# Roll of a matrix by 100 columns: head reads and stores with descriptors 4 rows apart

## The chip, the cores and the metric

One core of a Trainium2 chip runs the kernel. The metric is the device time of one execution in microseconds, from a median over runs; lower is better. A profile of one execution stands beside it.

## What is computed

```python
x = np.random.randn(8192, 8192).astype(np.float32)
np.roll(x, 100, axis=1)
```

Every row of 8192 float32 values (32,768 bytes) is rotated to the right by 100 columns. So `out[r, 100:]` is `x[r, :8092]`, and the first 100 columns of a row of the output are the last 100 of the same row of the input. Nothing is calculated; 268.4 MB are read and 268.4 MB are written.

## The kernel before

The shift is s = 100. The kernel rounds it up to a = 128 columns (512 bytes) and has g = a - s = 28. It splits each output row in two.

**The long copies.** Columns 128 to 8191 of the output are columns 28 to 8091 of the input. They go from HBM to HBM directly, in 16 transfers of 512 rows, 32,256 bytes to a row (line 31). Even transfers are issued from SP, odd ones from ACT, eight each, and none of them waits for anything that the kernel computes. Each issuing engine has a DMA queue of its own: in the profile q10 and q1. The 16 DMA engines serve both.

**The heads.** The first 128 columns of every output row take the last 100 columns and the first 28 columns of the same input row. These two pieces are not neighbours in that row, but the last 100 columns of row r-1 and the first 28 of row r are: in memory they are one run of 512 bytes. The kernel therefore reads runs of 512 bytes that straddle the row boundary, and VectorE sorts the pieces out in SBUF. The heads use the third DMA queue, q0, whose transfers POOL (GpSimd) issues.

The 8192 rows are treated in 8 stages of 1024 rows (`m = 8`, line 48; `n_st` = 8). In a stage, partition p of the 128 has the 8 neighbouring rows k\*1024 + p\*8 + j. For a stage k:

- The load on line 65 reads, for each partition, 8 runs of 512 bytes, one row (32 KiB) apart, into `t[:, :8, :]`. Slot j then holds the tail of row j-1 and the head of row j.
- The load on line 66 reads the missing tail, 400 bytes of the partition's last row, into slot 8. It is one descriptor to a partition.
- Stage 0 has no row ahead of it, and uses line 59 (8 tails of 400 bytes to a partition) and line 61 (8 heads of 112 bytes to a partition) in place of these.
- VectorE copies the tails (line 68) and the heads (line 70) from `t` into `h`, which then holds 8 finished runs of 512 bytes.
- The store on line 73 writes them to the 8 neighbouring output rows, again 32 KiB apart.

The order on POOL is loads of stage 0, loads of stage 1, store of stage 0, loads of stage 2, store of stage 1, and so on: a store stands behind the load issued after its own. The pools have a buffer for every stage, so no buffer is reused. POOL's stores wait for the VectorE copies, and the framework has eight completion semaphores for POOL's transfers, so that from the ninth transfer on each also waits for the one eight before it.

Of the kernel before, what the change touches and what calls it, by code (L numbers as in the profile page):

```python
# [1 line left out]

# [4 lines left out]


@with_exitstack
def kernel(  # L10
    ctx: ExitStack,
    tc: tile.TileContext,
    x: bass.AP,
    shift: int,
    out: bass.AP,
):
    nc = tc.nc
    n_rows, n_cols = x.shape
    s = shift % n_cols
    a = -(-s // 128) * 128  # L20
    g = a - s
    P = nc.NUM_PARTITIONS
    engines = [nc.sync, nc.scalar]
    n_chunks = 16
    rows = n_rows // n_chunks


    for i in range(n_chunks):
        r = slice(i * rows, (i + 1) * rows)
        if a < n_cols:  # L30
            engines[i % 2].dma_start(out=out[r, a:], in_=x[r, g:n_cols - s])
    if a == 0:
        return


    if a > 512:
        for i in range(n_chunks):
            r = slice(i * rows, (i + 1) * rows)
            nc.gpsimd.dma_start(out=out[r, :s], in_=x[r, n_cols - s:])
            if g > 0:  # L40
                nc.gpsimd.dma_start(out=out[r, s:a], in_=x[r, :g])
        return

    m = 8
    n_st = n_rows // P // m
    reads = ctx.enter_context(tc.tile_pool(name="reads", bufs=n_st))  # L50
    heads = ctx.enter_context(tc.tile_pool(name="heads", bufs=n_st))
    xt = x.rearrange("(k p j) c -> k p j c", j=m, p=P)
    ot = out.rearrange("(k p j) c -> k p j c", j=m, p=P)
    tiles = []
    for k in range(n_st + 1):
        if k < n_st:
            t = reads.tile([P, m + 1, a], x.dtype)
            if k == 0:
                nc.gpsimd.dma_start(out=t[:, 1:, :s], in_=xt[k, :, :, n_cols - s:])  # L59
                if g > 0:  # L60
                    nc.gpsimd.dma_start(out=t[:, :m, s:], in_=xt[k, :, :, :g])  # L61
            else:
                lead = bass.AP(tensor=x.tensor, offset=k * P * m * n_cols - s,
                               ap=[[m * n_cols, P], [n_cols, m], [1, a]])
                nc.gpsimd.dma_start(out=t[:, :m, :], in_=lead)  # L65
                nc.gpsimd.dma_start(out=t[:, m, :s], in_=xt[k, :, m - 1, n_cols - s:])  # L66
            h = heads.tile([P, m, a], x.dtype)
            nc.vector.tensor_copy(h[:, :, :s], t[:, 1:, :s])  # L68
            if g > 0:
                nc.vector.tensor_copy(h[:, :, s:], t[:, :m, s:])  # L70
            tiles.append(h)
        if k > 0:
            nc.gpsimd.dma_start(out=ot[k - 1, :, :, :a], in_=tiles[k - 1])  # L73


# [1 line left out]
_INS = ['x', 'shift']  # L77
_OUTS = [((8192, 8192), 'float32')]

_NUMBERS = {'shift': 100}  # L80


# [26 lines left out]
```

## Time and profile before

| | |
|---|---|
| median of 4 runs | 847.57 us (835.31 to 855.29) |
| the profiled execution's own time | 835.31 us |
| its span in the profile | 833.5 us |
| VectorE busy | 6.8 us, 16 instructions |
| POOL busy | 18.7 us, 28 instructions |
| bytes moved by the DMA engines | 272.99 MB, mean 328 GB/s |
| loads of stages 1 to 7 (line 65) | 7 of 512 KB, median 117.5 us from issue to landing |
| tails of stages 1 to 7 (line 66) | 7 of 50 KB, median 123.4 us |
| stores (line 73) | 8 of 512 KB, median 91.0 us |
| the last store issued | at 462.3 us |

The bytes of a transfer from HBM to HBM are counted once as moved, and as one read and one write of HBM. A queue's "share of 16 engines" is the time that its packets took, divided by 16 times the stretch looked at. A packet is what a DMA engine takes from a queue in one go: for the long copies it is one row of 32,256 bytes, for head loads and stores it is mostly 8 descriptors of 512 bytes, which is a partition's 4096 bytes. The 1.8 us between the profiled execution's time and its span lie around the span.

### The profile page before, as it was taken

The numbers are of one execution on the slowest core, as the hardware profiler recorded it, in microseconds if no ns is written. First come the engines' busy times: TensorE is split into PE (matmuls) and PEld (weight loads), VectorE is DVE, ScalarE is ACT, GpSimd is POOL, SyncE is SP. The second block draws the span as 40 slices with busy tenths as digits, with TensorE's granted clock in tenths as the row PEclk, the third lists the DMA queues.
The fourth block names the chain that finished last, engine by engine and source line by source line (L and its number), as shares of the span: only waits on it lengthen the run. The fifth ranks groups of instructions, "written<-read, shape, count | busy, mean of one in ns | idle before, by whom it ended". The sixth has DMA issues, their size and how long they took to land.

```text
span 833.5 us, 111 instructions
## 1 busy us (share of the span) xinstructions
DVE 6.8 (1%) x16; POOL 18.7 (2%) x28
## 2 busy tenths in 40 slices
DVE  0000000000000000000000000000000000000000
POOL 2001000000100100100000000000000000000000
DMA  9999999999999999999999999999999999999995
GB/s 297 343 340 325 336 345 333 337 335 336 328 334 334 339 332 335 337 332 335 330 341 335 339 327 338 327 322 327 333 324 327 325 325 324 325 327 324 324 327 200
DMA packets 10993, 272.99 MB, mean 328 GB/s; under 512 B 641, under 2 KB 641, under 8 KB 2801
## 3 DMA queue, kind: packets, MB, share of 16 engines
q10 hardware_dynamic: 4224, 132.12, 46.5%
q1 hardware_dynamic: 4224, 132.12, 46.4%
q0 software_dynamic: 2544, 8.75, 5.4%
q14 instruction: 1, 0.00, 0.0%
HBM read 268.79 MB, written 268.44 MB: 645 GB/s over the span
## 4 chain that ended last, share of the span: by engine, by line
another core or an unknown queue 35%; issue 15%; DMA 5%; DVE 1%; POOL 0%; POOLq 0%; PEldq 0%
DMA t<-in_x_dram 5%; DVE h L68 0%; POOL out_dram L73 0%; DVE h L70 0%; POOL t L59 0%; POOLq L104 0%; POOL t L66 0%; POOL t L65 0%; PEldq L104 0%; POOLq L73 0%
## 5 line engine op out<-in xcount | busy, mean ns | idle before, releaser
L73 POOL DMA_DIRECT2D out_dram<-h x8 | 6.9, 866 | 443.4 <-DVE h L68 406.5
L65 POOL DMA_DIRECT2D t<-in_x_dram x7 | 6.3, 894 | 0.0
L68 DVE COPY h<-t 128x800 f32<-128x800 f32 x8 | 4.6, 577 | 104.1 <-DMA t<-in_x_dram 104.1
L70 DVE COPY h<-t 128x224 f32<-128x224 f32 x8 | 2.2, 277 | 351.1 <-DMA t<-in_x_dram 351.1
L66 POOL DMA_DIRECT2D t<-in_x_dram x7 | 3.9, 563 | 0.0
L59 POOL DMA_DIRECT2D t<-in_x_dram x1 | 1.0, 1033 | 0.8 <-PEq L104 0.8
L61 POOL DMA_DIRECT2D t<-in_x_dram x1 | 0.9, 894 | 0.0
L90 POOL MEMSET const-float32-0.0<- 128x1 f32 x1 | 0.1, 100 | 0.2 <-issue 0.2
L90 POOL MEMSET const-bfloat16-1.0<- 128x1 bf16 x1 | 0.1, 103 | 0.0
L90 POOL MEMSET const-float32-1.0<- 128x1 f32 x1 | 0.1, 99 | 0.0
L90 POOL MEMSET const-uint8-127<- 128x1 uint8 x1 | 0.1, 99 | 0.0
## 6 DMA issues: line engine op xcount, KB each, us to landing
out_dram<-in_x_dram ACTq DMA_DIRECT2D x8, 16128.0 KB, 407.3
out_dram<-in_x_dram SPq DMA_DIRECT2D x8, 16128.0 KB, 408.2
out_dram<-h POOLq DMA_DIRECT2D x8, 512.0 KB, 91.0
t<-in_x_dram POOLq DMA_DIRECT2D x7, 512.0 KB, 117.5
t<-in_x_dram POOLq DMA_DIRECT2D x1, 400.0 KB, 30.6
t<-in_x_dram POOLq DMA_DIRECT2D x7, 50.0 KB, 123.4
t<-in_x_dram POOLq DMA_DIRECT2D x1, 112.0 KB, 39.5
```

The costliest lines, as they stand in the source:

```text
L59: nc.gpsimd.dma_start(out=t[:, 1:, :s], in_=xt[k, :, :, n_cols - s:])
L61: nc.gpsimd.dma_start(out=t[:, :m, s:], in_=xt[k, :, :, :g])
L65: nc.gpsimd.dma_start(out=t[:, :m, :], in_=lead)
L66: nc.gpsimd.dma_start(out=t[:, m, :s], in_=xt[k, :, m - 1, n_cols - s:])
L68: nc.vector.tensor_copy(h[:, :, :s], t[:, 1:, :s])
L70: nc.vector.tensor_copy(h[:, :, s:], t[:, :m, s:])
L73: nc.gpsimd.dma_start(out=ot[k - 1, :, :, :a], in_=tiles[k - 1])
L90: nc = _bacc.Bacc("TRN2", target_bir_lowering=False, num_devices=1)
```

## The change

The rows of the heads are dealt out in another way. There are 2 stages of 4096 rows in place of 8 of 1024. A partition has 32 rows, k\*4096 + p\*32 + j\*4 + q, with j from 0 to 7 and q from 0 to 3. One transfer moves one q: for each partition 8 runs that lie 4 rows (128 KiB) apart, and from partition to partition 32 rows (1 MiB), where it was 8 rows (256 KiB).

For q = 1, 2, 3 the straddling runs of 512 bytes are read (three loads to a stage, line 61 of the changed kernel). They hold the heads of rows 1 to 3 and the tails of rows 0 to 2 of each group of four. The tails of the fourth rows (400 bytes, line 62) and the heads of the first rows (112 bytes, line 65) are read straight into `h`. VectorE makes two copies to a stage, three times as large as before (lines 63 and 66). No special case for the first rows is left. All loads are issued ahead of all stores; then come 8 stores of 1024 rows each, one for each k and q (line 70). The long copies are untouched.

```diff
-    m = 8
-    n_st = n_rows // P // m
+    Q, J = 4, 8
+    n_st = n_rows // (P * Q * J)
...
-    xt = x.rearrange("(k p j) c -> k p j c", j=m, p=P)
-    ot = out.rearrange("(k p j) c -> k p j c", j=m, p=P)
+    xt = x.rearrange("(k p j q) c -> k q p j c", q=Q, j=J, p=P)
+    ot = out.rearrange("(k p j q) c -> k q p j c", q=Q, j=J, p=P)
     tiles = []
-    for k in range(n_st + 1):
-        if k < n_st:
-            t = reads.tile([P, m + 1, a], x.dtype)
-            if k == 0:
-                nc.gpsimd.dma_start(out=t[:, 1:, :s], in_=xt[k, :, :, n_cols - s:])
-                if g > 0:
-                    nc.gpsimd.dma_start(out=t[:, :m, s:], in_=xt[k, :, :, :g])
-            else:
-                lead = bass.AP(tensor=x.tensor, offset=k * P * m * n_cols - s,
-                               ap=[[m * n_cols, P], [n_cols, m], [1, a]])
-                nc.gpsimd.dma_start(out=t[:, :m, :], in_=lead)
-                nc.gpsimd.dma_start(out=t[:, m, :s], in_=xt[k, :, m - 1, n_cols - s:])
-            h = heads.tile([P, m, a], x.dtype)
-            nc.vector.tensor_copy(h[:, :, :s], t[:, 1:, :s])
-            if g > 0:
-                nc.vector.tensor_copy(h[:, :, s:], t[:, :m, s:])
-            tiles.append(h)
-        if k > 0:
-            nc.gpsimd.dma_start(out=ot[k - 1, :, :, :a], in_=tiles[k - 1])
+    for k in range(n_st):
+        t = reads.tile([P, Q - 1, J, a], x.dtype)
+        h = heads.tile([P, Q, J, a], x.dtype)
+        for q in range(1, Q):
+            lead = bass.AP(tensor=x.tensor, offset=(k * P * J * Q + q) * n_cols - s,
+                           ap=[[J * Q * n_cols, P], [Q * n_cols, J], [1, a]])
+            nc.gpsimd.dma_start(out=t[:, q - 1], in_=lead)
+        nc.gpsimd.dma_start(out=h[:, Q - 1, :, :s], in_=xt[k, Q - 1, :, :, n_cols - s:])
+        nc.vector.tensor_copy(h[:, :Q - 1, :, :s], t[:, :, :, :s])
+        if g > 0:
+            nc.gpsimd.dma_start(out=h[:, 0, :, s:], in_=xt[k, 0, :, :, :g])
+            nc.vector.tensor_copy(h[:, 1:, :, s:], t[:, :, :, s:])
+        tiles.append(h)
+    for k, h in enumerate(tiles):
+        for q in range(Q):
+            nc.gpsimd.dma_start(out=ot[k, q, :, :, :a], in_=h[:, q])
```

## The prediction

> **What bounds the kernel now.** I read the page's slices and queues first, since the kernel computes nothing.
>
> ```profile
> DMA  9999999999999999999999999999999999999995
> ...
> q10 hardware_dynamic: 4224, 132.12, 46.5%
> q1 hardware_dynamic: 4224, 132.12, 46.4%
> q0 software_dynamic: 2544, 8.75, 5.4%
> ...
> HBM read 268.79 MB, written 268.44 MB: 645 GB/s over the span
> ```
>
> The DMA engines are busy in every slice but the last. The heads (q0) are 8.75 of 273 MB and 5.4% of the engine time: 45.0 us on each of the 16 engines. The chain of waits doesn't help: it follows POOL and VectorE to 463 us and ends there, while the long copies run on to 833.5 with nothing waiting for them. So heads are hidden as a sequence; they can cost only what they take from the copies. Two resources could be short: the DMA engines' own time or HBM. I asked the DMA view for a stretch with heads (20 to 520 us) and for one without (540 to 800):
>
> ```profile
> DMA packets 7553, 167.57 MB, mean 335 GB/s; under 512 B 522, under 2 KB 522, under 8 KB 2621
> ## 3 DMA queue, kind: packets, MB, share of 16 engines
> q1 hardware_dynamic: 2535, 79.48, 45.7%
> q10 hardware_dynamic: 2535, 79.61, 45.7%
> q0 software_dynamic: 2483, 8.48, 8.4%
> ```
>
> ```profile
> DMA packets 2688, 84.64 MB, mean 326 GB/s; under 512 B 64, under 2 KB 64, under 8 KB 64
> ## 3 DMA queue, kind: packets, MB, share of 16 engines
> q10 hardware_dynamic: 1343, 42.29, 50.3%
> q1 hardware_dynamic: 1345, 42.35, 49.4%
> ```
>
> A copied byte is read from HBM and written to it, a head byte of a transfer touches HBM once. With heads: (2 x (79.48 + 79.61) + 8.48) / 500 us = 653 GB/s of HBM traffic. Without: 2 x 84.64 / 260 = 651. That is the same, although heads take 8.4% of the engines' time in the first stretch. The copy packets give way: 45.7% x 500 x 16 / 2535 = 1.44 us each with heads, 50.3% x 260 x 16 / 1343 = 1.56 without. HBM is the limit. The windows at the end confirm it (columns after the clock: DMA share, GB/s):
>
> ```profile
> 810.00:815.00 5.00, 0.00 (x0) 0.00 (x0) 1.00 0.95 323
> 815.00:820.00 5.00, 0.00 (x0) 0.00 (x0) 1.00 0.83 297
> 820.00:825.00 5.00, 0.00 (x0) 0.00 (x0) 1.00 0.59 252
> 825.00:830.00 5.00, 0.00 (x0) 0.00 (x0) 1.00 0.25 110
> 830.00:834.00 4.00, 0.00 (x0) 0.00 (x0) 1.00 0.04 16
> ```
>
> As engines run out of work, the others speed up: 252 / (0.59 x 16) = 26.7 GB/s an engine from 820 to 825, against 326 / 16 = 20.4 while all run. A copy packet could take 32,256 B / 26.7 = 1.21 us.
>
> Last, the price of a head packet, from a stretch that is mostly stores (470 to 520 us), then one that is mostly loads (180 to 200):
>
> ```profile
> q0 software_dynamic: 206, 0.72, 3.5%
> ```
>
> ```profile
> q0 software_dynamic: 98, 0.31, 12.0%
> ```
>
> Taking out the completion packets (41 and 21 under 512 B) leaves 3.5% x 50 x 16 / 165 = 0.17 us for a store packet and 12.0% x 20 x 16 / 77 = 0.50 us for a load packet.
>
> **What the Trainium skill says.** (1) HBM Reference, section "Specifications (TRN2)": about 716 GB/s for the two cores of a domain, and about 425 GB/s for a core streaming alone, bounded by its DMA engines. The trace agrees with both: 653 is 91% of the first, and 16 x 26.7 = 427 is the second. (2) DMA: Bandwidth & Descriptors, section "Queues, rings and completion order": an engine goes round its queues packet by packet. From 20 to 520 us there are 2483 head packets, some 2100 without completions, to 5070 copy packets, near the 1 to 2 of three full queues. (3) The same page, "Latency and other measured facts": row pitches at large powers of two cost rate: 207 GB/s each way at 512 KiB, 164 at 2 MiB, 103 at 4 and 8 MiB; the mechanism is an inference there. Before's trace shows nothing of a changed pitch. (4) The same page, "Specifications": below 512 B a transfer is read, modified and written. HBM's 268.44 MB written is just the output, so nothing extra is seen there.
>
> **The change part by part.**
>
> *Bytes.* Before, heads read 400 + 112 + 7 x (512 + 50) = 4446 KB; after, 2 x (3 x 512 + 400 + 112) = 4096 KB. Stores stay at 4096 KB. 350 KB less, 0.36 MB / 653 GB/s = **-0.55 us**.
>
> *Packets.* Before, 896 load packets of 4096 B (7 x 128), 1024 store packets and some 240 with small runs. After, 768, 1024 and about 256 (2048 descriptors of 400 B and 2048 of 112 B, in the packets of about 4 KB that lines 59 and 61 formed). At 0.50, 0.17 and, for small runs, again 0.50 (a choice): before 742 us, after 686, over 16 engines 46 and 43. Engine time isn't the limit, so these 3 us count **0**; if it were, -3.
>
> *Order and waits.* POOL issues 8 loads at once; the ninth and tenth wait for the first two to land (eight semaphores), then come the stores of stage 0, which wait for its loads and two VectorE copies. Those are 3 x 577 = 1.7 us and 3 x 277 = 0.8 us by their element counts. Nothing but head transfers queues behind these waits; the copies are issued from SP and ACT. Each engine has 2048 / 16 = 128 head packets, one to two copy packets. Such a turn carries 2 x 2 x 32,256 + 4096 = 133,120 B of HBM traffic, at 653 / 16 = 40.8 GB/s that is 3.26 us. Loads of both stages end near 64 x 3.26 = 209 us, stores near 418, where before's last store was issued at 462. Stores of stage 0 are ready near 105 us while stage 1's loads still fill the queue, so it doesn't run dry. Even if it did, there are 400 us of cover: **0**. Gone, it would cost the 100 us or so of one store round.
>
> *Pitch.* 32 KiB becomes 128 KiB inside a packet, 256 KiB becomes 1 MiB between partitions. Before has no row for it. Bounds: loads as cheap as stores, which HBM-bound gives 0 (engine-bound: first rival), and twice the price by the skill's fall from 207 to 103. I take **0**: a turn has 3.26 - 2 x 1.21 = 0.84 us for a head packet before the engine becomes the limit, and loads take 0.50.
>
> Sum on the profiled execution: 835.31 - 0.55 = 834.8. It stood 12.3 below the median, 847.57; carried to the median, **847.0 us**.
>
> **The rivals.**
>
> *Engine time sets the end (faster).* If load packets fell to the stores' 0.17 us at the new pitch and the engines were the limit, heads would take 128 x 0.17 = 22 us an engine in place of 45: -23, 824 us (-2.7%). For it: a DMA share of 1.00. Against: 653 and 651 GB/s.
>
> *Load packets become the bound (slower).* The wider pitch puts runs that are in flight together on fewer parts of HBM. Its place is the 64 load turns of each engine; the point is a load packet above 0.84 us, each 0.1 beyond costing 6.4 us. 2% (17 us) needs 0.84 + 17/64 = 1.11 us, 2.2 times now. The skill's factor of 2 gives 1.00: +10, 857. At 2.5 times, 1.25 us: +26, **873 us**. For it: loads are already three times as dear as stores. Against: the table's streams were the whole traffic, and heads are 3%.
>
> *The engines' ends spread otherwise.* From 810 us on, idle engine time is 0.05 x 5 + 0.17 x 5 + 0.41 x 5 + 0.75 x 5 + 0.96 x 3.5 = 10.3 us. Heads dealt out otherwise could take it away (837) or double it (857). Both lie within 2%.
>
> *The change doesn't do what it says.* The shape moves nothing, and only the order counts: 847 as well.
>
> **How the numbers follow.** Within 2% (831 to 865), which is about what a measurement of this kernel can tell from no change: 0.48, of which 0.35 for the flat sum and order and 0.13 for another spread of the ends; the likeliest case's own range is 837 to 857. Faster by over 2%: 0.20. Slower by over 2%: 0.32, more than faster, as it needs only the heads to go wrong and a gain needs HBM to go above 653. Half of the chance lies outside 2% because the pitch has no row in this trace. The range that leaves out 2 in 10 reaches from 827 to 874, into both rivals.
>
> **What would show it.** Right: HBM near 653 GB/s with and without heads, copies near 1.44 us beside heads, q0 near 5% and done by about 420 us, an HBM read of 268.4 MB. The slower rival: q0 well over 10%, fewer GB/s in the load half (to 209 us) alone. The faster one: load packets near 0.17 us and HBM above 660. I am wrong if the rate without heads, after 540 us, differs from 651: then the change acts through something that this profile doesn't show.

## The result and the profile after

The changed kernel takes 835.94 us (median of 43 runs, 830.61 to 844.78), the kernel before 845.74 (median of 64 runs, 833.43 to 855.65). The ratio is 0.9934 with a 95% interval of 0.9916 to 0.9952: a small gain, clear of noise, and within 2%. The ratio compares undisturbed runs only, those near the fastest of their kernel; since before's times are spread more widely, it shows less than the medians of all runs do, 835.94 / 845.74 = 0.988.

The two profiled executions must not be set against each other. Before's took 835.31 us, near the lowest of its 64 runs; after's took 838.69, above the median of its 43. They stand in the opposite order to the medians. The page of after, slices, queues and HBM traffic:

```profile
DMA  9999999999999999999999999999999999999996
...
q10 hardware_dynamic: 4224, 132.12, 47.5%
q1 hardware_dynamic: 4224, 132.12, 46.5%
q0 software_dynamic: 2336, 8.39, 4.6%
HBM read 268.44 MB, written 268.44 MB: 641 GB/s over the span
```

The heads take 4.6% of the engine time, 38.5 us an engine in place of 45.0, and 0.36 MB less is read, as worked out. The load half of the heads (40 to 200 us) and the stretch without heads (540 to 800) in the DMA view of after:

```profile
DMA packets 2388, 53.19 MB, mean 332 GB/s; under 512 B 128, under 2 KB 128, under 8 KB 828
## 3 DMA queue, kind: packets, MB, share of 16 engines
q10 hardware_dynamic: 796, 25.16, 44.7%
q1 hardware_dynamic: 796, 25.16, 43.0%
q0 software_dynamic: 796, 2.87, 11.6%
```

```profile
DMA packets 2659, 83.70 MB, mean 322 GB/s; under 512 B 64, under 2 KB 64, under 8 KB 64
```

HBM traffic is (4 x 25.16 + 2.87) / 160 = 647 GB/s in the first and 2 x 83.70 / 260 = 644 in the second. So HBM is again the limit with and without heads, and neither the fast nor the slow pitch rival shows: a load packet takes 11.6% x 160 x 16 / (796 - 96) = 0.42 us, against 0.50 before (96 of q0's packets are completions; the other 32 packets under 512 B are those of the long copies). What changed is the end of after (columns as before: DMA share and GB/s last):

```profile
810.00:820.00 10.00, 0.00 (x0) 0.00 (x0) 1.00 0.99 319
820.00:830.00 10.00, 0.00 (x0) 0.00 (x0) 1.00 0.76 316
830.00:837.00 7.00, 0.00 (x0) 0.00 (x0) 1.00 0.28 120
```

From 810 us to the end of the span an engine is idle for 0.1 + 2.4 + 0.72 x 7 = 7.5 us in the mean, against 10.3 in before. That is the difference between the mean engine's end and the last one's. This one pair doesn't explain a gain of 6 to 10 us, and 644 against 651 GB/s without heads points the other way. Experiments had to.

### The profile page after: what moved, and what is told of

Read it like the earlier page. It is cut to its first block, busy times and chain, and to the rows that moved or that the text cites. A ratio compares the mean times of both kernels' runs of the same rounds, so it can differ in the third digit from the quotient of the medians.

```text
span 836.9 us, 93 instructions
## 1 busy us (share of the span) xinstructions
DVE 3.7 (0%) x4; POOL 16.1 (2%) x22
## 3 DMA queue, kind: packets, MB, share of 16 engines
q0 software_dynamic: 2336, 8.39, 4.6%
HBM read 268.44 MB, written 268.44 MB: 641 GB/s over the span
## 5 line engine op out<-in xcount | busy, mean ns | idle before, releaser
L61 POOL DMA_DIRECT2D t<-in_x_dram x6 | 5.4, 910 | 0.8 <-PEq L101 0.8
L63 DVE COPY h<-t 128x2400 f32<-128x2400 f32 x2 | 2.8, 1410 | 213.4 <-DMA t<-in_x_dram 213.4
L62 POOL DMA_DIRECT2D h<-in_x_dram x2 | 1.8, 882 | 30.1 <-DMA t<-in_x_dram 30.1
L65 POOL DMA_DIRECT2D h<-in_x_dram x2 | 1.8, 882 | 29.5 <-DMA t<-in_x_dram 29.5
```

The lines of the kernel that those rows point to most:

```text
L61: nc.gpsimd.dma_start(out=t[:, q - 1], in_=lead)
L62: nc.gpsimd.dma_start(out=h[:, Q - 1, :, :s], in_=xt[k, Q - 1, :, :, n_cols - s:])
L63: nc.vector.tensor_copy(h[:, :Q - 1, :, :s], t[:, :, :, :s])
L65: nc.gpsimd.dma_start(out=h[:, 0, :, s:], in_=xt[k, 0, :, :, :g])
```

## The experiments

Twelve kernels were run in three jobs, each job on one chip with the kernel before among its runs. Times are compared within a job, as the jobs differ: before had a median of 846.29 us in the first, 834.14 in the second and 835.03 in the third.

A number that the views don't give is used beside them. Every transfer of the long copies ends with one small completion packet on each of the 16 engines; the time from the first to the last of these, read from the trace's packet records, tells how far the engines have drifted apart.

### The order alone

All 16 loads are issued ahead of the 8 stores; rows, tiles and transfers are those of before.

```diff
...
-        if k > 0:
-            nc.gpsimd.dma_start(out=ot[k - 1, :, :, :a], in_=tiles[k - 1])
...
+    for k, h in enumerate(tiles):
+        nc.gpsimd.dma_start(out=ot[k, :, :, :a], in_=h)
```

> The order alone: neighbouring rows and 8 stages as in the kernel before, but all 16 loads issued ahead of all 8 stores. Theory O (the gain comes from the order: full queue of loads, then of stores, done sooner): ratio to before about 0.993. Theory P (it comes from the pitch of 4 rows): 1.000. Theory E (the engines' ends spread less because the heads are dealt out otherwise): 1.000, with ends as in before.

0.9984 (0.9948 to 1.0020): the order gives nothing that can be told from noise, and theory O (0.993) falls. Its trace tells more. Its execution (854.94 us, in the upper half of its runs) ends like this:

```profile
810.00:820.00 10.00, 0.00 (x0) 0.00 (x0) 1.00 0.88 306
820.00:830.00 10.00, 0.00 (x0) 0.00 (x0) 1.00 0.40 171
830.00:840.00 10.00, 0.00 (x0) 0.00 (x0) 1.00 0.21 90
840.00:853.00 13.00, 0.00 (x0) 0.00 (x0) 1.00 0.12 50
```

For the last 23 us some two to four engines of 16 work alone (0.21 and 0.12 of 16). The drift of the SP transfers is 16.8 us at the first (about 105 us), 33.2 at the second, 47.6 at the third (about 314), then 48.0 and 47.1. It grows while the loads run, of which the last lands at about 314 us here, and stops with them. Stores and lone copies add none in this trace.

### The pitch alone

4 rows between descriptors, in 8 steps of 1024 rows, with stores between loads as in before.

```diff
...
+        prev = reads.tile([P, J, a], x.dtype)
+        nc.gpsimd.dma_start(out=prev[:, :, s:], in_=xt[k, 0, :, :, :g])
...
+            nc.vector.tensor_copy(h[:, :, :s], t[:, :, :s])
+            nc.vector.tensor_copy(h[:, :, s:], prev[:, :, s:])
+            prev = t
+            if pend is not None:
+                nc.gpsimd.dma_start(out=pend[0], in_=pend[1])
+            pend = (ot[k, q, :, :, :a], h)
...
```

> The pitch alone: 4 rows between descriptors as in the kernel after, in 8 steps of 1024 rows, a store behind the load issued after its own as in the kernel before. Theory O: 1.000. Theory P: 0.993, with load packets cheaper than 0.48 us. Theory E: 0.993 by engine ends closer together, HBM traffic with heads unchanged at about 650 GB/s.

0.9941 (0.9909 to 0.9972), 837.01 us: the gain of the change, without its order. The drift is 4.1 us at the first SP transfer and 9.1 at the third. HBM traffic beside the heads, 20 to 420 us, is (2 x (63.00 + 63.22) + 7.28) / 400 = 649 GB/s, unchanged. Theories P and E both foretold the ratio; the run with eight rows, below, tells them apart.

### No heads

> The heads are left out (the first 128 columns of the output are not written), the long copies alone. If heads cost only their HBM bytes, 8.75 MB / 653 GB/s = 13.4 us less, ratio 0.984. If the heads of before cost more than their bytes (all three theories), under 0.984: about 0.977 if the gain of the change is the removal of such an excess.

```diff
-    if a == 0:
-        return
+    return
```

0.9809 (0.9739 to 0.9879), 826.76 us. By the ratio before's heads cost 16 us (10 to 22), by the medians 846.29 - 826.76 = 19.5, where their bytes account for 13.4. So this run alone proves no excess. After's heads (835.90 us in this job, next run) cost 9.1, no more than their bytes, 8.39 MB / 650 GB/s = 12.9. Even without heads the engines drift: 1.8 us at the first SP transfer, 16.4 at the fifth.

### The kernel after again

The changed kernel, with no edit.

> The changed kernel again on the chip of the others: 0.993 by the result; also a second trace, for how HBM rate and engine ends differ between executions of the same kernel.

0.9913 (0.9887 to 0.9939), 835.90 us. The drift is 3.9 us at the first transfer and 21.0 at the last.

### Loads 4 rows apart, stores to neighbouring rows

The rows of `h` are put in the order of the output's rows; only the stores are shown.

```diff
...
-        for q in range(Q):
-            nc.gpsimd.dma_start(out=ot[k, q, :, :, :a], in_=h[:, q])
+        for i in range(4):
+            nc.gpsimd.dma_start(out=on[k, i, :, :, :a], in_=h[:, 2 * i:2 * i + 2].rearrange("p j q c -> p (j q) c"))
```

> Loads as in the kernel after (4 rows between descriptors), stores to 8 neighbouring rows of a partition (32 KiB apart, partitions 1 MiB apart). If the gain comes from loads that cost the engines unequal time (theory L): 0.992 as in the kernel after, ends within about 20 us. If the stores take part in it: 0.996 to 1.000.

1.0135 (1.0083 to 1.0187): slower, which no theory expected. While the loads run the drift is 2.2 and 4.5 us, as in after; while the stores run it grows to 26.5 at the fifth transfer. And these stores cost HBM rate. From 260 to 440 us, with stores only on q0, and then from 540 to 800 us of the same trace, without heads:

```profile
q1 hardware_dynamic: 876, 27.22, 48.8%
q10 hardware_dynamic: 881, 27.39, 46.0%
q0 software_dynamic: 876, 3.18, 5.4%
```

```profile
DMA packets 2733, 85.90 MB, mean 330 GB/s; under 512 B 70, under 2 KB 70, under 8 KB 70
```

That is (2 x 54.61 + 3.18) / 180 = 624 GB/s of HBM traffic in the first and 2 x 85.90 / 260 = 661 in the second. In after's trace of the result, the stretch from 260 to 440 us has (2 x (28.35 + 28.45) + 3.33) / 180 = 650, no less than its 644 without heads. So stores to neighbouring rows with partitions 1 MiB apart lower HBM traffic as a whole and add drift. The loads' share in the gain is not isolated by this run.

### Only the step between partitions

Before's order and its 8 neighbouring rows to a packet, but 32 rows from partition to partition, as in after.

```diff
-    xt = x.rearrange("(k p j) c -> k p j c", j=m, p=P)
-    ot = out.rearrange("(k p j) c -> k p j c", j=m, p=P)
+    xt = x.rearrange("(b p i j) c -> b i p j c", i=4, j=m, p=P)
+    ot = out.rearrange("(b p i j) c -> b i p j c", i=4, j=m, p=P)
...
-                lead = bass.AP(tensor=x.tensor, offset=k * P * m * n_cols - s,
-                               ap=[[m * n_cols, P], [n_cols, m], [1, a]])
+                lead = bass.AP(tensor=x.tensor, offset=(k // 4 * P * 4 * m + k % 4 * m) * n_cols - s,
+                               ap=[[4 * m * n_cols, P], [n_cols, m], [1, a]])
...
```

> The kernel before with its order and its 8 neighbouring rows to a packet, but partitions 32 rows (1 MiB) apart, where they were 8 rows (256 KiB). If what matters is the step between descriptors of one packet (theory D): 1.000, engine ends as uneven as before. If it is the step between partitions, and so what the 16 engines read at one time (theory G): 0.992.

1.0258 (1.0212 to 1.0303), 854.55 us. Neither theory foretold it (1.000 and 0.992): half of the change, alone, costs more than the whole gains. It was run again below.

### The heads alone

```diff
-        if a < n_cols:
+        if False:
```

> The heads of the kernel before alone; the long copies are left out (columns 128 to 8191 of the output are not written). If the neighbouring rows cost the engines unequal time by themselves, the engines' share of a load is uneven here: load packets of widely different length, about twice the spread of the kernel after. If the inequality needs the copies beside it, load packets are near the store packets' 0.16 us here, in both.

> The heads of the kernel after alone; the long copies are left out (columns 128 to 8191 of the output are not written). If the pitch costs HBM anything by itself, loads land sooner or later here than in the heads of the kernel before alone, per byte; if it needs the copies beside it, the two load rates agree within 10%.

One execution each: 41.60 us for the heads of before, 37.43 for those of after. The engine time of the heads, from the page of the first and of the second:

```profile
span 39.8 us, 91 instructions
...
q0 software_dynamic: 2544, 8.75, 74.3%
```

```profile
span 35.7 us, 73 instructions
...
q0 software_dynamic: 2336, 8.39, 83.6%
```

39.8 x 74.3% = 29.6 us and 35.7 x 83.6% = 29.8 us an engine: the same. All 16 engines finish each transfer within 2 us of each other in both. In these two executions the pitch costs the engines nothing by itself; its effect needs the long copies beside it. The packet records show where: data packets of the heads that take over 1 us.

| trace | packets over 1 us | over 2 us | time of those over 1 us on each engine |
|---|---|---|---|
| before, and again in the third job | 184, 171 | 34, 50 | 18.0, 18.3 us |
| order alone | 190 | 34 | 18.8 us |
| 1 MiB between partitions, second and third job | 165, 152 | 32, 43 | 16.0, 16.4 us |
| after, three traces | 101, 101, 104 | 0, 1, 0 | 7.7, 8.0, 8.0 us |
| pitch alone | 77 | 4 | 6.5 us |
| loads 4 rows apart, stores to neighbouring rows | 60 | 0 | 4.6 us |
| eight rows apart (below) | 132 | 1 | 10.3 us |
| heads alone, of before and of after | 6, 2 | 0, 0 | 0.5, 0.1 us |

The packets over 2 us tell the kernels apart best: 32 to 50 where neighbouring rows are loaded beside the copies, 0 to 4 elsewhere.

### Before, after and the partition step on one chip

> The kernel before, unchanged, for a second trace of it and for its time beside the others. Theory U (the neighbouring rows of the head loads hold some DMA engines back, by an amount that differs between executions and jobs, and the last engine sets the end): time minus the mean end of the engines is larger here the slower the execution is, while HBM traffic from 540 to 800 us stays near 650 GB/s. Rival theory H (HBM itself is slower in the slow executions): the mean end moves with the time.

> The kernel after, unchanged, on the chip of the kernel before and of the 1 MiB partitions. Theory U: 835 to 838, whatever the time of before, since little is left that can vary; if before is at 846 here 0.991, if at 834 about 1.000.

> The kernel before with partitions 32 rows apart again (8 neighbouring rows to a packet), now beside the kernel after, which has the same step between partitions but 4 rows between the descriptors of a packet. Theory D (the step inside a packet decides): slower than the kernel after by about 2%, as 854.6 against 836 on two chips. Theory C (the two chips differ, not the two kernels): within 0.5% of the kernel after.

These are the kernels of before, after and the partition step once more, unchanged. Before as a run of its own is at 0.9989 (0.9957 to 1.0022) of itself, 830.86 us. After is at 0.9912 (0.9880 to 0.9944), 823.31 us. It was expected at 835 to 838, with a ratio of about 1.000 beside a before as fast as this one; so after moves with the chip as before does. The partition step is at 1.0310 (1.0251 to 1.0368), 856.63 us: 33 us from after on the same chip. Theory C falls. Theory D holds in kind, with 4% where it had about 2%.

The ends of the three, before (842.53 us, near the top of its runs of 824.44 to 843.18, whose median is 830.86), after (821.40) and the partition step (857.46):

```profile
790.00:800.00 10.00, 0.00 (x0) 0.00 (x0) 1.00 0.97 323
800.00:810.00 10.00, 0.00 (x0) 0.00 (x0) 1.00 0.82 316
810.00:820.00 10.00, 0.00 (x0) 0.00 (x0) 1.00 0.49 210
820.00:830.00 10.00, 0.00 (x0) 0.00 (x0) 1.00 0.31 132
830.00:841.00 11.00, 0.00 (x0) 0.00 (x0) 1.00 0.10 44
```

```profile
790.00:800.00 10.00, 0.00 (x0) 0.00 (x0) 1.00 0.97 323
800.00:810.00 10.00, 0.00 (x0) 0.00 (x0) 1.00 0.84 313
810.00:820.00 10.00, 0.00 (x0) 0.00 (x0) 1.00 0.40 174
```

```profile
820.00:830.00 10.00, 0.00 (x0) 0.00 (x0) 1.00 0.52 226
830.00:840.00 10.00, 0.00 (x0) 0.00 (x0) 1.00 0.43 184
840.00:850.00 10.00, 0.00 (x0) 0.00 (x0) 1.00 0.22 94
850.00:856.00 6.00, 0.00 (x0) 0.00 (x0) 1.00 0.04 16
```

Before's engines start to run dry at the same time as after's, near 800 us, and its last one works 21 us longer. The idle time from 790 us on is 0.3 + 1.8 + 5.1 + 6.9 + 9.7 = 23.8 us in before (span end 840.8) and 0.3 + 1.6 + 5.6 = 7.5 in after (span end 819.6). So 16.3 of the 21.2 us between these two spans are drift; a typical execution of before is some 12 us shorter and probably holds less of it. HBM traffic without heads, 540 to 800 us, before and then after:

```profile
DMA packets 2709, 85.03 MB, mean 327 GB/s; under 512 B 73, under 2 KB 73, under 8 KB 73
```

```profile
DMA packets 2719, 85.64 MB, mean 329 GB/s; under 512 B 64, under 2 KB 64, under 8 KB 64
```

It is 2 x 85.03 / 260 = 654 GB/s in before and 2 x 85.64 / 260 = 659 in after. That leaves 5 us to HBM, the 0.5 of the saved bytes among them. Before's own two traces, on two chips, point the same way: the span of 840.8 us is 7.2 longer than that of 833.5, its idle time 13.5 us more (23.8 and 10.3), so its mean engine ended earlier. Theory U is borne out for the larger part of this pair; theory H has a small one.

Summed from the packet records of every trace, the idle time from 790 us on is 20 to 26 us in four of the five with neighbouring rows in both loads and stores and 9.5 in the fifth, before at 835.31 us; it is 4.5 to 8.1 in the five with 4 or 8 rows, and 7.4 without heads. (The views' rounded shares give up to 0.9 us more.) So against after's 6.6 to 8.1 the drift is worth only some 1 to 3 us in an execution as fast as that fifth one. What it is worth in before's typical execution no trace shows.

The partition step pays twice. Its idle time is of before's size, and it is slower beside the heads. 20 to 500 us, the partition step first and then before:

```profile
q1 hardware_dynamic: 2390, 75.03, 46.8%
q10 hardware_dynamic: 2386, 74.90, 45.4%
q0 software_dynamic: 2322, 7.91, 7.7%
```

```profile
q1 hardware_dynamic: 2449, 76.87, 45.9%
q10 hardware_dynamic: 2444, 76.71, 45.8%
q0 software_dynamic: 2395, 8.19, 8.2%
```

(2 x 149.93 + 7.91) / 480 = 641 GB/s against (2 x 153.58 + 8.19) / 480 = 657: 2.4% over the 530 us that the heads last, some 13 us.

### Eight rows apart

```diff
-    Q, J = 4, 8
+    Q, J = 8, 8
```

> The kernel after with 8 rows (256 KiB) between descriptors and 64 rows (2 MiB) between partitions, one stage of 8192 rows. If a wider step goes on evening out the engines: 0.990 of before where after is at 0.991, at best the no-heads time plus the heads' bytes, 826.8 + 12.9 = 839.7 or less. If 4 rows are a sweet spot: slower than the kernel after by over 0.5%.

0.9929 (0.9903 to 0.9956), 825.50 us, beside after's 0.9912 on the same chip. The intervals overlap: a wider step gains nothing more, and 4 rows are no sharp optimum. No version tried here beats the changed kernel. The heads' line of its page:

```profile
q0 software_dynamic: 2320, 8.39, 5.6%
```

Its heads take 5.6% of 820.8 us, 46 us an engine, as much as before's 45.0, and it gains nearly what after gains. So theory P's reason, cheaper load packets, falls, and theory E stands: not the mean cost of the heads decides, but how unequally it falls on the engines.

The drift of the engines (first to last completion of an SP transfer, us) over all traces used:

| kernel | 1st transfer | 3rd | 5th | last |
|---|---|---|---|---|
| before, 835.31 us | 10.8 | 17.4 | 18.4 | 23.9 |
| before, third job, 842.53 | 12.6 | 37.7 | 57.9 | 44.1 |
| order alone, 854.94 | 16.8 | 47.6 | 47.1 | 39.1 |
| 1 MiB between partitions, second job, 854.59 | 13.9 | 34.1 | 46.8 | 35.7 |
| 1 MiB between partitions, third job, 857.46 | 17.0 | 42.4 | 50.8 | 47.0 |
| after, 838.69 | 4.8 | 10.3 | 15.6 | 15.9 |
| after, again in the first job, 838.68 | 3.9 | 11.9 | 16.9 | 21.0 |
| after, third job, 821.40 | 3.9 | 6.1 | 9.1 | 15.8 |
| pitch alone, 834.55 | 4.1 | 9.1 | 10.2 | 10.7 |
| loads 4 rows apart, stores to neighbouring rows, 843.73 | 2.2 | 12.7 | 26.5 | 23.1 |
| eight rows, 822.59 | 3.8 | 6.4 | 9.0 | 9.1 |
| no heads, 827.02 | 1.8 | 8.5 | 16.4 | 15.6 |

Every kernel that loads neighbouring rows stands at 10 us or more after the first transfer, even in the first line, one of before's fastest executions; every kernel that loads with 4 or 8 rows between descriptors is under 5 there and, where its stores have that step too, no more than 6 us above the kernel without heads from then on.

The packet records name no engine, but they can be sorted by engine: a packet mostly starts within 5 ns of the end of the one ahead of it, an engine takes one packet of each queue in turn, and each engine has 32 rows and one completion of every long transfer. Sorted so, the time that the heads take on the engine that ends first and on the one that ends last is:

| trace | ends first: end, heads (packets over 1 us) | ends last | correlation of heads and end over the 16 |
|---|---|---|---|
| before, third job | 796 us, 26 us (1) | 840 us, 66 us (20) | 0.96 |
| 1 MiB between partitions, third job | 808 us, 32 us (4) | 854 us, 63 us (19) | 0.96 |
| before, 835.31 us | 808 us, 39 us (8) | 832 us, 45 us (9) | 0.67 |
| after, third job | 803 us, 38 us (6) | 818 us, 33 us (4) | -0.03 |

In before's third-job trace the last engine ends 44 us after the first, and 39 us of that is time of its own head packets. Every packet over 1 us is a load. Engines that run in step can be taken for one another, so the last two rows are less sure than the first two.

## Why the prediction was right, and where it was off

- **HBM bounds the kernel, with heads and without.** Right: 647 and 644 GB/s in after, 657 and 654 in before's second trace.
- **Bytes.** Right: HBM reads 268.44 MB. The 0.55 us are too few to be told apart.
- **Order and waits count nothing.** Right, by the order alone (0.9984). The time at which the heads end was off: 418 us was foretold, and the last head packet of after's trace is at 474. The turn of 3.26 us was right, and the count of turns was not. From 40 to 200 us each of the three queues gives 796 packets, and 96 of q0's are completions, which the prediction left out; so a completion takes a turn of its own. That makes 2336 / 16 = 146 turns to an engine, not 128, and 146 x 3.26 = 476 us. The cover of hundreds of us made this harmless.
- **Pitch counts nothing.** This is the step that failed. The prediction set the mean price of a load packet, 0.50 us, against 0.84 us of room in the mean turn, and concluded that engine time costs nothing. The room is there in the mean, but it isn't shared: every engine has its own 32 rows of each long transfer, whose completions lie up to 57.9 us apart, so an engine that is held back keeps most of its debt to the end. Neighbouring rows as in before have 34 to 50 packets of over 2 us, 4 rows apart 0 to 4, and the four engines that end last in before's third-job trace hold 69 of its 171 over 1 us. Mean prices hide such a tail. (The price of a store packet, 0.17 us, is 0.16: of the 41 small packets taken out, 10 were the long copies'. Nothing rests on it.)
- **The rivals.** The third one, that the engines' ends spread otherwise, is what happened: it gave 837 us and 835.94 were measured. That the two are so close is partly luck: the 837 took away all of the 10.3 us of idle time, of which 7.5 are left in after's trace. Its chance was 0.13, too low, since the trace at hand showed 10.3 us of idle time at the end and came from one of the fastest executions; the second trace of before shows 23.8. The engine-time rival (824) mistook the limit, and load packets stayed far from 0.17 us. The slower rival is refuted for this change: 0.42 us, not more than before. A step of 1 MiB between partitions can cost: with neighbouring rows in a packet it takes 2.4% of HBM traffic and 3.1% of the time. But it doesn't do so by dear load packets, as the rival had it: sorted out as above, they take 0.45 us in the mean there, and 0.46 in before on that chip. The last rival, that only the order counts, is refuted by the order alone (0.9984) and the pitch alone (0.9941).
- **The sign of being wrong.** The rate without heads was not to differ from 651 GB/s. It is 644 in after, but also 644 in the kernel without heads, 654 in before's second trace and 659 in after's third. So the sign was set tighter than executions agree, and it decides nothing.
- **The Trainium skill's row pitches.** DMA: Bandwidth & Descriptors, "Latency and other measured facts", has the rate fall with wider pitch. It was measured on copies between HBM tensors. Here 1 MiB in place of 256 KiB between partitions hurts with neighbouring rows in a packet (1.0310) and not with 4 rows (0.9912), nor do 2 MiB with 8 rows (0.9929). For these heads the pitch between partitions alone doesn't tell the rate.
- **The forecast.** 847.0 us against 835.94, inside the range, and within 2% as forecast, but below the likeliest case's own 837 to 857. Of the 11.1 us, 1.8 lie in the base, a median of 4 runs (847.57) where 64 gave 845.74. The rest is the one zero, which should have been some 9 us by the medians and 5 by the ratio.

What stays open: why neighbouring rows beside the copies make some load packets take up to 3.6 us, why more of them on some engines than on others, and why that differs between executions. Nothing here shows the parts of HBM that an address falls on.

## What to carry to other kernels

When transfers are dealt out to the DMA engines in advance and HBM is the limit, look at the last 5% of the span: the idle share there is what the slowest engine costs, and small transfers early on can cause it without touching the mean rate. A single trace of a kernel whose runs differ by 2% may be of its best execution; ask how its time stands to the median before a cost is taken from it. Change the step inside a packet and the step between partitions apart from each other, as they can act in opposite ways.

## What the runs showed that was not expected

The same kernel differs by 1.5% between chips or jobs (before: 846.29, 834.14 and 835.03 us; after: 835.90 and 823.31), more than the change is worth. After's HBM traffic without heads was 644 GB/s in the trace of the result and 659 in the third job's; no head packet runs in that stretch, so this part doesn't lie with the heads. The ratio of after to before held: 0.9934, 0.9913 and 0.9912.
